# A two-layer diffusion backbone on one core: constant products ahead of the first stage, weights stored by partition, and value products with the softmax sum in one bank

## The chip, the cores and the metric

The kernel runs on one core of a Trainium2 chip. The metric is the device time of one execution in microseconds (us). Three runs of the kernel before took 1395.3, 1395.98 and 1396.6 us, so the median is 1395.98 us.

## What is computed

The input is a latent stream `x` of 1024 tokens, a context of 256 tokens, both 1024 wide in fp32, and a conditioning vector. Two layers follow, and an RMS norm at the end. Each layer normalises its input, scales and shifts it by a modulation vector (a product of the conditioning with a 1024 x 3072 matrix), projects it, runs attention, multiplies by a SiLU gate and projects back.

```python
mod_x = (silu_c @ w_mod[i] + b_mod[i])
hx = rms_norm(x, norm_g[i]) * (1.0 + sc_x) + sh_x
# layer 0: 16 query heads on 4 key/value heads, q and k normed, rotary positions on latent tokens
s = jnp.einsum('bqkgd,bskd->bkgqs', qi, k_all).astype(jnp.float32) * ATTN_SCALE
p = jax.nn.softmax(s, axis=-1)
o = jnp.einsum('bkgqs,bskd->bqkgd', p, v_all)
yx = (o * jax.nn.silu(z)) @ w_out
# layer 1: 16 heads, an 8 x 16 neighbourhood with a learned bias, and the context keys
x = x + g_x * yx
```

Layer 0 also updates the context, with attention among the context tokens alone. In the title and in the kernel "layer one" of the change is this layer 0, the grouped attention.

## The kernel before, in words

Tokens stand in ten tiles of 128: t = 0 to 7 are latent, 8 and 9 context. To keep fp32 accuracy each fp32 operand is split into a high and a low fp16 part, and each product is made of three fp16 products (high by high, high by low, low by high) that add up in PSUM.

**First stage.** `mod_cols(kt)` loads one column block of the modulation matrix (four DMAs into two tiles `wm`, in runs of 128 floats), multiplies it by the conditioning (`pm`, L552), copies the result (`mrow`, L554), turns it into columns (`pmc`, L557) and leaves scale `acol` (L558) and shift `scol` (L560). `ln_pre(t)` loads a token tile and divides it by its root mean square. `h_kt(t0, n, kt)` transposes n tiles of block kt on TensorE (L791), applies scale and shift on ScalarE into an fp32 tile `tf` (L793), casts that to the high part on VectorE (L796) and subtracts for the low part (L797). `kv_mm` (L801) makes the key and value projection: 24 products of 512 columns for each token tile. Tiles 0 to 3 go through kt = 0 to 7 together, each in a PSUM bank of its own; tiles 4 to 9 follow. `kv_post` norms and rotates the keys and writes `k1`, `k2`, `v1`. In `v1` each head has 64 high columns, one column with a constant (for the softmax sum) and 64 low columns.

**Layer 0.** A pair u of heads goes through `a_proj` (q and gate, L917; the q tiles are transposed by DMA, L934, two token tiles at a time, and copied, L936), then `a_att` and, for u = 0 to 3 and the latent tiles, also `q_att` for the second head. `a_att` has keys on the partitions, needs a row of maxima beforehand (`mgen`, `rows`), and multiplies probabilities by values in `pv_mm`: for each key tile and each of up to four query tiles, three products: high by `v[0:65]` (L1014), high by `v[65:129]` (L1015), low by `v[0:65]` (L1016). `o_evict` divides by the sum (L992 to L996). `q_att` has queries on the partitions; it takes its sums from the accumulator of the Exp on ScalarE (L1086), transposes its probabilities by DMA (L1088), multiplies by 128 value columns (L1094) and 64 (L1096), and finishes with a reduction, a copy, an addition and four scaled products (L1105 to L1112). `o_out` splits the head pair's output and transposes each part by its own DMA (L1027). `mod_block` computes the other modulation vectors (L571, L579) spread over the layer.

**Layer 1** loads its weights in `b_load` (64 DMAs, in runs of 128 floats, L1304), projects (`b_qk` L1322, `b_vz` L1355, L1358), runs attention in `b_att` and finishes each half of a head in `fin` (L1446 to L1456), which also calls `o_out`. `b_out` ends the kernel (L1527).

**Order.** All DMAs but four small ones are issued by SyncE (SP), one after the other. The function calls of the program only set a first rank. The class `Planner` gives each instruction a cost, builds the dependences between tiles, simulates the five engines, derives due times and repeats that five times; the best order that it finds is then fixed on every engine. On each engine the chip runs the instructions in that order, and so does the SP queue.

Of the kernel before, what the change touches and what calls it, by code (L numbers as in the profile page):

```python
# [21 lines left out]
P = 128  # L22
# [20 lines left out]
class Planner:  # L43
# [42 lines left out]
    def cost(self, x, rd, wr):  # L86
# [67 lines left out]
    def graph(self):  # L154
        acc = {}
        self.pred = []
        self.node = []
# [11 lines left out]
        for x in self.ins:  # L169
# [11 lines left out]
            p = set()  # L181
# [29 lines left out]
            self.pred.append(p)  # L211
        self.eng = [self.ENG[x.engine.name] for x in self.node]
# [42 lines left out]
    def schedule(self, key=None, margin=0.0, scale=None):  # L255
# [4 lines left out]
        succ = [[] for _ in range(N)]  # L260
        npred = [0] * N
        for i, ps in enumerate(self.pred):
            npred[i] = len(ps)
            for p in ps:
                succ[p].append(i)
        rdy = [0.0] * N
# [143 lines left out]
        self.order, self.start, self.done, self.succ, self.came = order, start, done, succ, came  # L410
        return max(done)

    def deadlines(self, margin):
# [14 lines left out]
        for i in sorted(range(N), key=lambda i: -start[i]):  # L428
            e, d = self.eng[i], done[i] - start[i]
            for j in self.succ[i]:  # L430
                due[i] = min(due[i], due[j] - (0.0 if self.eng[j] == e == "PE" else d + self.SEM[self.eng[j]] + margin))
            for j in heirs.get(i, ()):
# [46 lines left out]
def trunk_kernel(ctx, tc, x, cx, cc, norm_g, ng_row, b_cols, sel_c, w_mod, b_mod, a_w_in, a_qg, a_kg, a_w_out,  # L479
                 b_w_in, rpb, b_w_out, fin_g, cos_t, sin_t, mask_q, out):  # L480
# [17 lines left out]
    def ps_pv(name):  # L498
        return psum.tile([P, 4, 65], F32, name=name, tag="pv", bufs=2)
# [41 lines left out]
    def mod_cols(kt, pool):  # L541

        tiles = []
        for j in range(2):
            wm = pool.tile([P, 4, 2, P], F32, name=f"wm{kt}{j}", tag="wm", bufs=7)
# [3 lines left out]
            tiles += [wm[:, d] for d in range(4)]  # L549
        ps = ps_mx(f"pm0{kt}", shape=(P, 2, P))  # L550
        for d in range(KT):
            T.matmul(ps[32 * (d % 4):32 * (d % 4) + 32], s2[:, d, :], tiles[d], start=d < 4, stop=d >= 4)  # L552
        row = lp.tile([P, 2, P], F32, name=f"mrow{kt}", tag="mrow", bufs=1)
        V.tensor_copy(row, ps)  # L554
        pc = ps_mx(f"pmc0{kt}", shape=(P, 2, 2))
        for r in range(2):
            T.matmul(pc[:, r, :], row[:, r, :], sel, start=True, stop=True)  # L557
        V.tensor_scalar(acol[0][:, kt, :], pc[:, 1, :], hg[:, 0, kt:kt + 1], gb[:, 0, kt:kt + 1], op0=ALU.mult,  # L558
                        op1=ALU.add)
        V.tensor_scalar(scol[0][:, kt, :], pc[:, 0, :], 0.5, bsc[:, 0, 0, kt:kt + 1], op0=ALU.mult, op1=ALU.add)  # L560

    def mod_block(pool, l, c0):
# [4 lines left out]
        for hf in range(2):  # L567
            wm = pool.tile([P, KT // 2, 512], F32, name=f"wg{nm}{hf}", tag="wg", bufs=1)
            for i in range(KT // 2):
                kt = hf * KT // 2 + i  # L570
                DM.dma_start(wm[:, i], w_mod[l, kt * P:(kt + 1) * P, c0:c0 + 512])  # L571
                yield 1.0
# [93 lines left out]
    oc_hi = yp.tile([P, KT, NC * P], F16, name="oc_hi")  # L666
    oc_lo = yp.tile([P, KT, NC * P], F16, name="oc_lo")
# [31 lines left out]
    def norm_rope_split(pool, sqs, psv, alt, nt, nh, t0, gc, gs, gplain, nm):  # L699
# [29 lines left out]
        q16 = pool.tile([P, 4, 2, HD], F16, name="q16" + nm, tag="q16", bufs=2)  # L729
# [16 lines left out]
    def a_src(kt0, nk, ncol):  # L746
# [869 lines left out]
```

## Time and profile before

| | |
|---|---|
| median of three runs | 1395.98 us |
| profiled execution, own time | 1397.8 us |
| its span, first to last instruction | 1396.0 us |
| TensorE (PE) busy | 1341.6 us, 96% |
| weight loads (PEld) busy | 930.8 us, 67% |
| VectorE (DVE) busy | 1000.0 us, 72% |
| ScalarE (ACT) busy | 938.8 us, 67% |
| GpSimd (POOL) busy | 648.5 us, 46% |
| queue of SP: packets, MB | 433544, 178.66 |

Busy is the time in which at least one instruction of the engine was under way. Products on TensorE overlap: the next begins while the one before still drains, so the distance between two starts, not the duration of one, is what a product costs in a full stream. 1.8 us of the profiled execution lie outside its span.

### The profile page before, as it was taken

To read this page: it belongs to the slowest core of one execution; us is meant where nothing else is said; L and a number is where in the kernel's file an instruction comes from. 1 tells how busy PE (TensorE), PEld (TensorE's weight loads), DVE (VectorE), ACT (ScalarE), POOL (GpSimd) and SP (SyncE) were. 2 spreads that over 40 slices of the span, in tenths; PEclk is the share of its full clock that TensorE was granted. 3 is DMA by queue.
4 is the path that set the end of the run, shared out by engine and by line. 5 is a ranking of instruction groups with operands and counts; after the bars stand their busy time and mean duration, and the time that the engine had idled before them with its cause. 6 is when DMAs were issued, how large, how long until landed. Compare 5 with 4: busy or idle time off the path is not lost.

```text
span 1396.0 us, 35447 instructions
## 1 busy us (share of the span) xinstructions
PE 1341.6 (96%) x13402; PEld 930.8 (67%) x13402; DVE 1000.0 (72%) x2568; ACT 938.8 (67%) x2294; POOL 648.5 (46%) x907
## 2 busy tenths in 40 slices
PE   4899999999999999999999999999999999999897
PEld 2458777777777777776654476867677686867443
DVE  2697878888789787689347756677776768687733
ACT  2463889888979777788742437677777767686811
POOL 2132778776867766687864301312122222322332
PEclk9999999999999999999999999999999999999999
DMA  8754468778676223234438735585666766597832
GB/s 258 234 125 118 98 120 134 141 151 159 139 142 136 70 62 70 57 111 109 104 97 192 188 97 114 94 157 122 128 136 116 144 112 148 97 170 149 172 109 103
DMA packets 434294, 180.97 MB, mean 130 GB/s; under 512 B 340225, under 2 KB 412865, under 8 KB 434121
## 3 DMA queue, kind: packets, MB, share of 16 engines
q1 hardware_dynamic: 433544, 178.66, 58.5%
q8 instruction: 105, 1.72, 0.5%
q14 instruction: 69, 0.56, 0.1%
q10 hardware_dynamic: 576, 0.03, 0.0%
HBM read 87.36 MB, written 12.08 MB: 71 GB/s over the span
## 4 chain that ended last, share of the span: by engine, by line
PE 56%; DVE 8%; ACT 5%; issue 3%; DMA 2%; POOL 0%; DVEq 0%; POOLq 0%; ACTq 0%; SPq 0%
PE pvz L1355 11%; PE poa L1236 7%; PE pa L917 7%; PE pb L1322 6%; PE pob L1527 5%; PE st L1143 3%; PE st L1144 2%; PE pm L947 2%; PE pv L1015 2%; PE pv L1014 2%; PE pv L1016 2%; PE bpv L1435 1%; ACT bpf L1426 1%; PE pvz L1358 1%; DVE bmx L1413 1%
## 5 line engine op out<-in xcount | busy, mean ns | idle before, releaser
L1008 POOL TENSOR_TENSOR pl<-pf,ph 128x256 f16<-128x256 f32 x400 | 273.6, 708 | 77.7 <-ACT pf L1130 61.9
L1008 POOL TENSOR_TENSOR bph<-bpf,bph 128x256 f16<-128x256 f32 (+1 forms) x128 | 99.6, 789 | 314.5 <-ACT bpf L1426 245.8
L917 PE MATMUL pa<-wa,x 128*128 128x256 f16 x1536 | 220.3, 272 | 1.0 <-DVE q16q L731 0.6
L1322 PE MATMUL pb<-hb_hi,wb 128*128 128x512 f16 (+1 forms) x640 | 191.4, 358 | 0.7 <-DVE bq L1337 0.7
L1128 ACT ACTIVATE ph<-st 128x512 f16<-128x512 f32 x240 | 143.9, 603 | 59.2 <-PE st L1144 56.2
L1355 PE MATMUL pvz<-wb,hb_hi 128*128 128x256 f16 x1024 | 174.8, 273 | 4.9 <-DVE bk L1341 3.3
L917 PEld LDWEIGHTS <-x 128*128 128x128 f16 x1536 | 140.0, 97 | 33.6 <-issue 2.5
L948 DVE TENSOR_REDUCE mxp<-pm 128x1 f32<-128x512 f32 x192 | 128.8, 684 | 25.9 <-PE pm L947 24.9
L1130 ACT ACTIVATE pf<-st 128x512 f32<-128x512 f32 x240 | 144.4, 605 | 0.3
L1322 PEld LDWEIGHTS <-wb 128*128 128x128 f16 x960 | 92.9, 98 | 75.0 <-issue 1.3
L1355 PE MATMUL pvz<-wb,hb_lo 128*128 128x256 f16 x512 | 139.7, 273 | 0.0
L1015 PE MATMUL pv<-v,ph 128*128 128x64 f16 x960 | 123.8, 195 | 0.0
L1014 PE MATMUL pv<-v,ph 128*128 128x65 f16 x960 | 123.4, 193 | 0.0
L1016 PE MATMUL pv<-v,pl 128*128 128x65 f16 x960 | 122.1, 192 | 0.6 <-POOL pl L1008 0.6
L1355 PEld LDWEIGHTS <-hb_hi 128*128 128x128 f16 x1024 | 97.1, 98 | 29.2 <-DVE bk L1341 5.1
L1008 POOL TENSOR_TENSOR qpp<-qpf,qpp 128x256 f16<-128x256 f32 (+1 forms) x158 | 93.7, 617 | 47.7 <-ACT qpf L1086 35.3
L1322 PE MATMUL pb<-hb_lo,wb 128*128 128x512 f16 (+1 forms) x320 | 114.6, 358 | 0.0
L1014 PEld LDWEIGHTS <-ph 128*128 128x128 f16 x960 | 90.9, 97 | 20.8 <-issue 0.6
L1015 PEld LDWEIGHTS <-ph 128*128 128x128 f16 x960 | 90.4, 97 | 15.2
L1016 PEld LDWEIGHTS <-pl 128*128 128x128 f16 x960 | 91.2, 99 | 10.9 <-POOL pl L1008 1.6
L1424 ACT ACTIVATE bph<-bpf,bnx 128x384 f16<-128x384 f32 (+1 forms) x128 | 68.6, 581 | 39.1 <-DVE bnx L1416 38.9
L1143 PE MATMUL st<-q,k 128*128 128x512 f16 x240 | 90.9, 379 | 0.9 <-ACT pf L1130 0.7
(261 smaller groups left out, 3678.9 us busy)
## 6 DMA issues: line engine op xcount, KB each, us to landing
wg<-in_w_mod SPq DMA_DIRECT2D x64, 256.0 KB
wsb<-in_b_w_in SPq DMA_DIRECT2D x64, 256.0 KB
wm<-in_w_mod SPq DMA_DIRECT2D x32, 256.0 KB
wsa<-in_a_w_in SPq DMA_DIRECT2D x64, 128.0 KB
xstage<-in_x SPq DMA_DIRECT2D x8, 512.0 KB
wsoa<-in_a_w_out SPq DMA_DIRECT2D x16, 256.0 KB
x<-in_x SPq DMA_DIRECT2D x8, 512.0 KB
x_d<-x SPq DMA_DIRECT2D x8, 512.0 KB
```

The lines of the kernel that those rows point to most:

```text
L917: T.matmul(ps[:, :, i, :], hA(a, kt, t), wt[w][:, kt, :], start=n == 0, stop=n == 3 * KT - 1)
L948: V.tensor_reduce(mxs[i][:, t, ch:ch + 1], pm, axis=AX.X, op=ALU.max)
L1008: G.tensor_tensor(lo[:, c], p32[:, c], hi[:, c], op=ALU.subtract)
L1014: T.matmul(pv[:, t, :], hi[:, c], v[:, 0:65], start=first and t == 0, stop=False)
L1015: T.matmul(pv[:, t, 0:HD], hi[:, c], v[:, 65:129], start=False, stop=False)
L1016: T.matmul(pv[:, t, :], lo[:, c], v[:, 0:65], start=False, stop=last and t == n - 1)
L1128: S.activation(ph, st, AF.Exp)
L1130: S.activation(p32, st, AF.Exp)
L1143: T.matmul(so, k1[:, g, kc], q1[:, :, i, :], start=True, stop=False)
L1236: T.matmul(ps, lhs(a, kt), w[b][:, kt, :], start=n == 0, stop=n == 3 * KT - 1)
L1322: T.matmul(ps[:, 0:n].rearrange("p (t q) -> p t q", q=P), wt[a][:, kt, which * P:(which + 1) * P], hb[b][:, c0 // P:(c0 + n) // P, kt], st ...
L1355: T.matmul(ps[:, :, j, :], hb[a][:, t, kt], wt[w][:, kt, 256:512], start=m == 0, stop=m == 3 * KT - 1)
```

## The change

The weights are laid out beforehand so that each partition reads one long run. The first stage works on tile 4 together with tiles 0 to 3 (three blocks behind), and computes the modulation of later blocks ahead. 34 products of a constant tile stand in front of it. `h_kt` writes the high part directly from ScalarE and makes an fp32 copy on VectorE from PSUM. In layer 0 the accumulator of a query tile takes a place of 129 columns (65 for the fourth), so that high by `v[0:129]` is one product; `q_att` uses the same products and takes its sum from the constant column. High and low parts are transposed by one DMA where there were two, and from u = 1 on four q tiles by one. The planner's cost of a DMA falls by 15%, and a second DMA into the same tile no longer waits, in the plan, for the first to land.

```diff
@@ Planner.cost, graph
-            return (430.0 if len(list(outs[0].ap)) < 3 else 550.0), m * 4 / ro * (11 + ro * 0.0432) / 16
+            return (430.0 if len(list(outs[0].ap)) < 3 else 550.0), m * 4 / ro * (11 + ro * 0.0432) / 16 * 0.85
...
-                            p.add(r[1])
+                            (o if self.ENG[x.engine.name] == self.ENG[self.node[r[1]].engine.name] == "SP"
+                             else p).add(r[1])
@@ mod_cols: split into load, quarters, cols
-            for r in range(2):
-                a = w_mod[0, 4 * j * P:4 * j * P + P, r * D + kt * P:r * D + kt * P + 1]
-                DM.dma_start(wm[:, :, r, :], bass.AP(a.tensor, a.offset, [[3 * D, P], [P * 3 * D, 4], [1, P]]))
+                DM.dma_start(wm, w_m0[kt, :, 4 * j:4 * j + 4])
@@ mod_block
-                DM.dma_start(wm[:, i], w_mod[l, kt * P:(kt + 1) * P, c0:c0 + 512])
+                DM.dma_start(wm[:, i:i + 2], w_mb[n, :, kt:kt + 2])
@@ first stage
+    ones = lp.tile([P, 512], F16, name="ones")
+    V.memset(ones, 1.0)
+    idle = ps_mx("idle")
+    for n in range(34):
+        T.matmul(idle, ones[:, 0:P], ones, start=n == 0, stop=n == 33)
@@ h_kt
-        S.activation(tf[:, 0:n], ps, AF.Identity, scale=acol[0][:, kt, s:s + 1], bias=scol[0][:, kt, s:s + 1])
-        V.tensor_copy(hi[:, kt, c], tv)
-        V.tensor_tensor(lo[:, kt, c], tv, hi[:, kt, c], op=ALU.subtract)
+        S.activation(hi[:, kt, c], pv, AF.Identity, scale=a, bias=b)
+        V.tensor_scalar(tf, pv, a, b, op0=ALU.mult, op1=ALU.add)
+        V.tensor_tensor(lo[:, kt, c], tf, hi[:, kt, c], op=ALU.subtract)
@@ main loop of the first stage
+    LAG = 3
+    for kt in range(KT + LAG):
+        if kt + 2 < KT:
+            loads(kt + 2)
...
+        if kt < KT:
+            kv_mm(banks[0], 0, kt)
+        if kt + 1 < KT:
+            mod[kt + 1][2]()
+            h_kt(0, 4, kt + 1)
+        if kt < KT:
+            for t in range(1, 4):
+                kv_mm(banks[t], t, kt)
+        if kt + 2 < KT:
+            mod[kt + 2][1]()
+        if kt >= LAG:
+            h_kt(4, 1, kt - LAG)
+            kv_mm(banks[4], 4, kt - LAG)
+        if kt >= KT:
+            kv_post(banks[kt - KT], kt - KT)
+        if kt >= 5:
+            h_kt(5, 3, kt - 5)
@@ a_load
-            load_w(wa[u], a_src(2 * j, 2, [u * P, 1536 + u * P]), 2 * j, 2, 256, f"a{u}{j}")
+            load_w(wa[u], a_src(a_wq[u, :, 2 * j:2 * j + 2].rearrange("p k r c -> p (k r c)")), 2 * j, 2, 256, f"a{u}{j}")
@@ b_load
-                DM.dma_start(st.rearrange("p (r c) -> p r c", c=P),
-                             bass.AP(a.tensor, a.offset, [[4 * D, P], [D, 4], [1, P]]))
+                DM.dma_start(st, b_wp[u, :, kt].rearrange("p r c -> p (r c)"))
@@ a_proj.post
+            if u and b in (0, 2):
+                return
+            c = slice(0 if u else 2 * (b % 2), 2 * (b % 2) + 2)
@@ o_evict
+        lo = pool.tile([P, 3, HD], F32, name="olo" + nm, tag="olo", bufs=1)
+        S.copy(lo[:, 0:m], pv_cols(pv, HD + 1, m, HD))
+        V.tensor_tensor(pv_cols(pv, 0, m, HD), pv_cols(pv, 0, m, HD), lo[:, 0:m], op=ALU.add)
@@ pv_mm
-            T.matmul(pv[:, t, :], hi[:, c], v[:, 0:65], start=first and t == 0, stop=False)
-            T.matmul(pv[:, t, 0:HD], hi[:, c], v[:, 65:129], start=False, stop=False)
-            T.matmul(pv[:, t, :], lo[:, c], v[:, 0:65], start=False, stop=last and t == n - 1)
+        o = 129 * t
+        if t < 3:
+            T.matmul(pv[:, o:o + 129], hi, v[:, 0:129], start=first, stop=False)
+        else:
+            T.matmul(pv[:, o:o + 65], hi, v[:, 0:65], start=first, stop=False)
+            T.matmul(pv[:, o:o + HD], hi, v[:, 65:129], start=False, stop=False)
+        T.matmul(pv[:, o:o + 65], lo, v[:, 0:65], start=False, stop=last)
@@ o_out
-            for dst, src in ((hi, oh), (lo, ol)):
-                DM.dma_start_transpose(dst[:, c].rearrange("p (t q) -> p t q", q=P),
-                                       src[:, 0:n].rearrange("p t f -> p (t f)"))
+            DM.dma_start_transpose(dst.rearrange("p t a q -> p (t a) q"), oo[:, 0:n].rearrange("p t a f -> p (t a f)"))
@@ q_att
-                S.activation(pf, pf, AF.Exp, bias=nmx, accum_out=sums[:, t, c:c + 1])
+                S.activation(pf, pf, AF.Exp, bias=nmx)
...
-        V.tensor_reduce(sm, sums, axis=AX.X, op=ALU.add)
-        V.tensor_scalar_mul(sm, sm, 2.0 * WS * WS)
-        V.reciprocal(sm, sm)
...
-        S.copy(oc, pv[:, :, HD:P])
-        V.tensor_tensor(oc, pv[:, :, 0:HD], oc, op=ALU.add)
-        for t in range(4):
-            V.scalar_tensor_tensor(og[:, t, HD:P], oc[:, t], sm[:, t:t + 1], sz[:, t, HD:P], op0=ALU.mult, op1=ALU.mult)
+        o_evict(aq, pv, og, 4, sz, 0, 1, f"q{u}{pt_}")
@@ b_att.fin
-                    for t in range(4):
-                        V.scalar_tensor_tensor(og[:, t, i * HD:(i + 1) * HD], oc[:, t], sm[:, t:t + 1],
-                                               sz[:, hf * 4 + t, i * HD:(i + 1) * HD], op0=ALU.mult, op1=ALU.mult)
+                    V.tensor_tensor(oc, oc, sm.unsqueeze(2).broadcast_to([P, 4, HD]), op=ALU.mult)
+                    V.tensor_tensor(og[:, :, i * HD:(i + 1) * HD], oc, sz[:, hf * 4:hf * 4 + 4, i * HD:(i + 1) * HD],
+                                    op=ALU.mult)
```

## Rows read from the trace of the kernel before

**Rows 1.** Busy time of each engine by stage: stretch, length, PE, PEld, DVE, ACT, POOL.
```profile
117.00:450.00 333.00, 323.43 (x3992) 249.62 (x3990) 275.05 (x766) 269.51 (x625) 237.17 (x362) 1.00 0.68 134
450.00:690.00 240.00, 238.83 (x3181) 175.06 (x3179) 176.31 (x370) 189.76 (x380) 179.87 (x254) 1.00 0.35 86
...
800.00:1300.00 500.00, 491.69 (x4489) 360.20 (x4487) 359.91 (x1026) 354.25 (x1024) 120.42 (x169) 1.00 0.65 129
```

**Rows 2.** The chain that ended last: start, length, what (two of its pieces).
```profile
718.88 64.55 PE poa L1236 x299
...
839.25 2.68 PE pvz L1358 x48
```

**Rows 3.** PE in order of time in the first stage: start, length, line.
```profile
11.79 0.69 PE L791 MATMUL pl<-idf,xstage 128*128 128x128 f32 x2 [11.79 <-DVE ms_ln L604]
...
26.14 4.60 PE L801 MATMUL pkv<-wkv,x 128*128 128x512 f16 x11
...
61.19 1.07 PE L552 MATMUL pm<-wm,s 128*32 128x256 f32 x16
...
62.81 0.61 PE L557 MATMUL pmc<-sel,mrow 128*128 128x2 f32 x4 [0.18 <-DVE ms_ln L604]
63.27 2.75 PE L801 MATMUL pkv<-wkv,x 128*128 128x512 f16 x12
65.86 0.71 PE L791 MATMUL pl<-idf,xstage 128*128 128x128 f32 x5
...
100.33 0.39 PE L811 MATMUL pkt<-id,q16k 128*128 128x128 f16 x4
...
109.41 0.60 PE L917 MATMUL pa<-wa,x 128*128 128x256 f16 x4
```

**Rows 4.** Stretches of 10 us in the first stage: columns as in rows 1, then clock, DMA share, GB/s.
```profile
10.00:20.00 10.00, 5.13 (x27) 2.40 (x28) 3.87 (x9) 3.56 (x8) 2.21 (x4) 1.00 1.08 313
...
50.00:60.00 10.00, 7.93 (x44) 3.85 (x45) 5.50 (x15) 6.50 (x11) 1.96 (x3) 0.83 1.07 371
...
90.00:100.00 10.00, 10.00 (x58) 5.38 (x57) 9.88 (x32) 6.22 (x15) 3.05 (x3) 1.00 0.32 87
```

**Rows 5.** PE in order of time in layer 0: nine value products and what follows.
```profile
506.15 0.19 PE L1014 MATMUL pv<-v,ph 128*128 128x65 f16 x1
...
506.43 0.38 PE L947 MATMUL pm<-k,q 128*128 128x512 f16 x1
```

**Rows 6.** Groups by line and form: count, busy us, mean ns, idle before.
```profile
L1453 DVE SCALAR_TENSOR_TENSOR bog<-boc,bse,bsz 128x64 f32<-128x64 f32 x128 | 37.5, 341 | 0.2
L1086 ACT ACTIVATION_READ_ACCUMULATOR qpf<-qpf,qnx 128x1 f32 x96 | 19.6, 204 | 0.0
L1240 DVE TENSOR_TENSOR tm<-poa,gt 128x512 f32<-128x512 f32 x20 | 13.8, 688 | 18.5 <-PE poa L1236 18.4
L1450 ACT COPY boc<-bpv 128x256 f32<-128x256 f32 x32 | 12.0, 374 | 15.8 <-PE bpv L1437 15.7
L1112 DVE SCALAR_TENSOR_TENSOR og<-qoc,qse,sz 128x64 f32<-128x64 f32 x32 | 11.7, 408 | 0.0
L994 DVE TENSOR_TENSOR pv<-pv,ors 128x256 f32<-128x256 f32 x24 | 10.2, 427 | 0.4
L796 DVE CAST x<-tf 128x512 f16<-128x512 f32 x16 | 8.4, 525 | 4.7 <-ACT tf L793 4.6
```

**Rows 7.** Who waited for whom: total us, times, longest (whole span; SP queue among them).
```profile
PEld L1094 <- DMA qpp<-qpp: 7.1, 9, 1.9
...
SPq L1304 <- DVE bv L1366: 25.9, 2, 25.7
...
SPq L548 <- PE pm L552: 14.8, 5, 5.3
```

**Rows 8.** SP in order of time in layer 0: start, length; first and last of 40.
```profile
347.14 1.22 SPq L1027 DMA_TRANSPOSE oa<-oh  x1
...
394.34 1.20 SPq L1027 DMA_TRANSPOSE oc_hi<-oh2c  x1
```

More of the change, by code (lines that the diff above doesn't have):

```diff
@@ L156, in graph @@
         self.pred = []
+        self.after = []
         self.node = []
@@ L260, in schedule @@
         succ = [[] for _ in range(N)]
+        late = [[] for _ in range(N)]
         npred = [0] * N
         for i, ps in enumerate(self.pred):
-            npred[i] = len(ps)
+            npred[i] = len(ps) + len(self.after[i])
             for p in ps:
                 succ[p].append(i)
+            for p in self.after[i]:
+                late[p].append(i)
         rdy = [0.0] * N
@@ L409, in schedule @@
                     offer(j)
-        self.order, self.start, self.done, self.succ, self.came = order, start, done, succ, came
+            for j in late[i]:
+                rdy[j] = max(rdy[j], s)
+                npred[j] -= 1
+                if not npred[j]:
+                    offer(j)
+        self.order, self.start, self.done, self.succ, self.late, self.came = order, start, done, succ, late, came
         return max(done)
@@ L498, in ps_pv @@
     def ps_pv(name):
-        return psum.tile([P, 4, 65], F32, name=name, tag="pv", bufs=2)
+        return psum.tile([P, 512], F32, name=name, tag="pv", bufs=2)
     idf = main.tile([P, P], F32, name="idf")
@@ L562, in mod_block, with load, quarters @@
-    def mod_block(pool, l, c0):
+        def load():
+            for j in range(2):
+                wm = pool.tile([P, 4, 2, P], F32, name=f"wm{kt}{j}", tag="wm", bufs=7)
+                DM.dma_start(wm, w_m0[kt, :, 4 * j:4 * j + 4])
+                tiles.extend(wm[:, d] for d in range(4))
+        def quarters():
+            ps = ps_mx(f"pm0{kt}")
+            pm = ps[:, 0:2 * P].rearrange("p (a b) -> p a b", a=2)
+            for d in range(KT):
+                T.matmul(pm[32 * (d % 4):32 * (d % 4) + 32], s2[:, d, :], tiles[d], start=d < 4, stop=d >= 4)
+            row = lp.tile([P, 2, P], F32, name=f"mrow{kt}", tag="mrow", bufs=1)
+            V.tensor_copy(row, pm)
+            tiles[:] = [ps, row]
@@ new lines, in cols @@
+        def cols():
+            ps, row = tiles
+            pc = ps[:, 2 * P:2 * P + 4].rearrange("p (a b) -> p a b", a=2)
+            for r in range(2):
+                T.matmul(pc[:, r, :], row[:, r, :], sel, start=True, stop=True)
+            V.tensor_scalar(acol[0][:, kt, :], pc[:, 1, :], hg[:, 0, kt:kt + 1], gb[:, 0, kt:kt + 1], op0=ALU.mult,
+                            op1=ALU.add)
+            V.tensor_scalar(scol[0][:, kt, :], pc[:, 0, :], 0.5, bsc[:, 0, 0, kt:kt + 1], op0=ALU.mult, op1=ALU.add)
@@ L564, in mod_block @@
+        return load, quarters, cols
+    def mod_block(pool, n, l, c0):
         nm = f"{l}{c0}"
@@ L842, in trunk_kernel @@
     tc.swap_default_side()
-    for kt in range(KT):
-        h_kt(4, 4, kt)
-        if kt % 2:
-            kv_post(banks[kt // 2], kt // 2)
+    for kt in range(KT + LAG - 5, KT):
+        h_kt(5, 3, kt)
+    for t in range(3, 5):
+        kv_post(banks[t], t)
     wa = {}
@@ L861, in trunk_kernel @@
         if t < NX:
-            for kt in (2 * t - 8, 2 * t - 7):
+            for kt in range((8, 11, 14)[t - 5] - 8, (11, 14, 16)[t - 5] - 8):
                 h_kt(8, 2, kt)
@@ L1058, in q_att @@
         pend = []
-        pv = psum.tile([P, 4, P], F32, name=f"qpv{u}{pt_}", tag="pv", bufs=2)
-        sums = aq.tile([P, 4, 3], F32, name=f"qsm{u}{pt_}", tag="qsm", bufs=2)
+        pv = ps_pv(f"qpv{u}{pt_}")
         og = og_of(u, pt_)
```

185 lines of the change are left out of this document (87 added, 98 removed).

## The prediction

> **What bounds it now.** I read the busy times by stage first [rows 1]. In both attention stages of layer 0 and in layer 1 TensorE is busy for 97 to 99% of the stretch, every other engine less: 9.6 us are open at 117 to 450 us, 1.2 at 450 to 690, 8.3 in layer 1. So I asked whether a busy TensorE is a full one. In the chain that ended last, 299 products of 512 columns take 64.55 us, 0.216 each, and 48 of 128 columns 2.68 us, 0.056 each [rows 2]: one distance between starts, column by column, with nothing in between. There TensorE bounds the kernel, and only fewer columns or fewer products help.
>
> The Trainium skill, "Trainium Kernel Development and Optimization", section Performance Expectations, says that matmul busy time is a bad metric, and that the busy share of weight loads is a good one. By that, with weight loads at 75% of the stretch from 117 to 450 us, a quarter of TensorE's time would be free, the term for value products below would be 0, and the time 1374 instead of 1369. I go by the starts.
>
> The first stage is different. The first product starts at 11.79 us, and layer 0's projection at 109.41 [rows 3]. TensorE's own work in it, at full rate: 240 key and value products at 0.216 = 51.8 us; 80 transposes at 0.11 (five of them take 0.71, of which 0.27 is the last one's length) = 8.8; eight modulation blocks at 1.07 and their columns at 0.61 = 13.4; ten key transposes of 0.39, some 0.25 of it before the next product, = 2.5. That is 76.5 us of 109.4; 33 are lost. Three losses show. Nothing runs until 11.8 us. Eleven products then take 4.60 us, 0.43 each, the 1.2 GHz level, where later twelve take 2.75 [rows 3]. And block by block TensorE waits for modulation, ScalarE and VectorE, while loads wait in turn for `pm` to free their buffers, 14.8 us [rows 7]: the DMAs move 313 and 371 GB/s where they run [rows 4], but don't run throughout.
>
> **The change, part by part.**
>
> *First stage.* The constant products need no load. 34 of them take 7.3 us at 0.216 or 14.6 at 0.43; from about 1 us they end between 8.5 and 15.6. I take 12.5, as a part of them runs at the lower level. By then the first modulation block (1 MB), the first token tile (0.5 MB) and the first weights (0.25 MB) have landed: 1.75 MB at 313 GB/s are 5.6 us, behind some 2 us of issue. Real work starts near 13 us. Loads are no bound after that: until the last block 8.4 MB of modulation weights, 4.2 of tokens and 2.1 of projection weights are 14.7 MB, 47 us at 313 and 40 at 371 GB/s, while TensorE's eight steps of the loop (1.68 modulation, 0.55 transposes, 15 x 0.216 products = 5.5 us) take 44. With 76.5 us of work and no loss the stage would end at 89.5. I add 3.5 us for waits, as each block still passes TensorE, VectorE, TensorE, VectorE and ScalarE one after the other, now a step ahead of its use: **93 instead of 109.4, -16.4 us**. Bounds: 87.5 (work from 11, no loss, -22) and 103 (VectorE, first rival, -6). VectorE gets more work here: the cast of 525 ns gives way to a pass from PSUM like the 688 of L1240 [rows 6], 0.16 more for each of 16 blocks of four tiles and about as much again for smaller pieces, some 4 us. What hides it is TensorE's own loop; VectorE is busy 9.88 of 10 us at 90 to 100 us [rows 4], so that cover is thin.
>
> *Value products of layer 0.* Nine take 0.28 us, 0.093 for three [rows 5]. A product of 129 columns costs 0.056 by rows 2, one of 65 a third of 0.093, so two cost 0.087: 6 ns less. Three products become two in 240 key tiles x 3 query tiles and 16 x 2 x 2 of the context, 784 times: -4.9 us. In `q_att` the first three query tiles cost one column more, nothing; the fourth takes three products for two, 80 times 6 ns = +0.5. **-4.4 us**, on TensorE's full stream. Bounds: 0 (129 columns as dear as the two they replace) and -8.
>
> *Evictions and sums.* `q_att` loses 96 accumulator reads of 204 ns on ScalarE, 19.6 us, and, per block, four products of 408 ns against two of 427 [rows 6] on VectorE, eight times. All 40 evictions of `a_att` gain a copy and an addition: about 0.32 and 0.36 us for 192 columns by the 374 and 427 of 256 columns, 24 times, and some 0.27 and 0.29 for 128, 16 times: 25 us in all, half on each engine. I cost it at nothing: two PSUM banks take turns, and TensorE has the products of the other one and the projections. If that cover is gone, all 25 us return and the time is near 1394. ScalarE's balance in the first half, where it is busiest, is better by over 10 us; that shortens waits only where TensorE waits, so nothing is booked.
>
> *DMA queue.* In layer 0 the SP queue is nearly always issuing: 40 issues in the 48 us from 347.14 on, a transpose 1.2 us whatever its size [rows 8]. Gone are 14 of 40 transposes of q and 21 of 42 of outputs (14 in layer 0's latent part, 7 in the context's), 42 us of issue time, and 78 shorter issues: 14 copies of q, 32 of 64 weight loads and 32 of 64 modulation loads. What waits for the queue now is `q_att`'s value product, 7.1 us [rows 7]. I take **-4 us**, between 0 and -7.1, since buffers also hold the queue. q tiles 0 and 1 now leave with tiles 2 and 3; the maxima of all four were needed by the same row of maxima before, so nothing further waits for it.
>
> *Layer 1.* Four products of 341 ns [rows 6] become two of about 0.42, 32 times: 17 us less of VectorE; 14 fewer transposes, and longer runs for 64 loads. TensorE is open for 8.3 us here [rows 1]. I take **-2 us**, between 0 and -8.3.
>
> **Sum.** The profiled execution took 1397.8 us: -16.4 - 4.4 - 4 - 2 = -26.8 gives 1371.0. It lies 1.8 above the median of the runs, so the forecast is 1369 us. All lower bounds together give 1350, all upper ones 1390.
>
> **Rivals.**
>
> *VectorE bounds the first stage.* It is full at 90 to 100 us already, 9.88 of 10 [rows 4], with some 4 us to come. Against: it idles half of the first 60 us, which the loop now fills. The stage ends at 103: 10.4 us more, 1379.
>
> *The clock falls again.* The constant products raise it, but TensorE then waits for loads and for its first block. For: it was granted 0.83 at 50 to 60 us, after TensorE had waited between blocks [rows 4]. At 0.43 a product until about 30 us, some 8 us are lost: 1377. The Trainium skill, "TensorE: Matmul & The Clock Gate", HAM oscillation, says that waits for DMA throttle TensorE anew; by that page constant products that end before the loads land are in vain. The 0.83 agrees.
>
> *The head start is lost.* Layer 0 begins earlier, but keys of the last tiles wait for VectorE, and TensorE runs out of projection work: 16 us come back, with the other terms halved 1390. Against: 25 us of projection stand between.
>
> *Slower: a load at the head of the queue.* The plan now lets a second DMA into a tile go at once and holds transfers cheaper, so it may put weight loads earlier. On the chip a load whose buffer is still read holds every later transpose. The nearest price: L1304 waited 25.7 us once [rows 7]. TensorE has some 2 us of value products pending, so each such wait within attention costs about 24. From two on the gain is gone: 1369 + 48 = 1417. Against: the longest waits now fall where nothing hangs on the queue.
>
> **How the numbers follow.** Forecast 0.64, its own range 1358 to 1381; VectorE 0.14; clock 0.09; head start 0.06; queue 0.07. From 1356 to 1388 lie nearly nine tenths of the first and the next two, some 0.8. Within 0.2% (2.8 us, about what a measurement of this kernel can tell from no change) lies half of the head start's case: 0.03. Faster: 0.90; slower: 0.07.
>
> **What would show it.** Right: layer 0's projection starts near 93 us; products at 0.216 from about 12 us on; three value products in 0.087 us; `q_att` waits less than 4 us for transposes; layer 1's fins lose 17 us of VectorE. Wrong: VectorE full and TensorE open at 60 to 100 us; value products of 129 columns well over 0.06; waits of PE for evictions, or a long wait of a load at the head of SP while transposes stand behind it.

## The result, and the profile after

The changed kernel takes **1383.4 us** (median of four runs, 1381.65 to 1386.41) against 1395.64 for the kernel before: a ratio of 0.9914, 95% interval 0.9895 to 0.9932. The forecast was 1369, with a range from 1356 to 1388: the sign and the range held, the gain is 12 us instead of 27. One execution of the kernel before in the series below (1746.55 us) and one of the changed kernel (1872.02 us) ran at a lower granted clock (0.75 and 0.73) and are left out of every median and ratio. The profiled execution took 1382.83 us with a span of 1381.0, 15.0 us shorter than the span before.

The first stage, PE in order of time (start, length, line):

```profile
1.47 10.39 PE L772 MATMUL idle<-ones 128*128 128x512 f16 x34 [1.47 <-DVE twos L552]
11.70 0.38 PE L807 MATMUL pl<-idf,xstage 128*128 128x128 f32 x2
...
93.56 5.27 PE L965 MATMUL pa<-wa,x 128*128 128x256 f16 x46
...
116.68 1.01 PE L999 MATMUL pm<-k,q 128*128 128x512 f16 x2 [2.38 <-issue]
...
121.21 0.38 PE L1191 MATMUL st<-q,k 128*128 128x512 f16 x1
```

Layer 0's projection starts at 93.56 us instead of 109.41 [rows 3]: the 15.8 us are there. Ahead of 116.68 TensorE has waited 2.38 us, the first long wait of the projection. Stretches of 10 us (columns as in [rows 4]) show what the stage now runs against:

```profile
10.00:20.00 10.00, 8.02 (x67) 4.29 (x66) 6.28 (x20) 5.06 (x10) 1.41 (x2) 1.00 1.03 408
50.00:60.00 10.00, 7.82 (x42) 3.97 (x40) 9.38 (x22) 8.43 (x19) 6.95 (x6) 1.00 0.54 71
60.00:70.00 10.00, 9.72 (x57) 5.25 (x57) 9.94 (x26) 5.79 (x13) 2.32 (x3) 1.00 0.60 157
90.00:100.00 10.00, 10.00 (x82) 7.39 (x80) 9.44 (x24) 5.30 (x13) 3.47 (x4) 1.00 0.38 120
110.00:120.00 10.00, 7.53 (x51) 5.47 (x50) 4.92 (x12) 1.47 (x4) 1.01 (x1) 0.83 0.75 114
```

First the loads are full (DMA share 1.03, 408 GB/s), then VectorE is (9.4 to 9.9 of 10 us); the clock falls at the wait near 115 us. The stages after that, with the columns of [rows 1], are as full as they were, 323.87 and 238.23 us of TensorE against 323.43 and 238.83:

```profile
117.00:450.00 333.00, 323.87 (x3741) 246.81 (x3743) 271.89 (x746) 268.64 (x550) 234.34 (x358) 0.99 0.65 130
450.00:690.00 240.00, 238.23 (x2751) 171.12 (x2740) 176.72 (x380) 193.42 (x398) 183.49 (x259) 1.00 0.30 84
...
800.00:1300.00 500.00, 491.98 (x4544) 364.01 (x4545) 359.50 (x996) 360.06 (x1045) 127.14 (x172) 1.00 0.65 131
```

Where did the head start go? Layer 1's first product, in the kernel before and then in the changed one (PE in order of time):

```profile
793.61 0.38 PE L1322 MATMUL pb<-hb_hi,wb 128*128 128x512 f16 x1
```
```profile
784.21 0.38 PE L1372 MATMUL pb<-hb_hi,wb 128*128 128x512 f16 x1
```

From the first projection to here, layer 0 took 793.6 - 109.4 = 684.2 us before and 784.2 - 93.6 = 690.6 after: **+6.4, where -8.4 was forecast**. From here to the end of the span it is 602.4 before and 596.8 after, -5.6. So -15.8 + 6.4 - 5.6 = -15.0.

For layer 0 I use one account throughout. For every product, the time by which the next one starts later than the median distance of its form counts as **waits** (over 12 ns, at full clock) or as **clock** (at the lower one); the rest is the **stream**, what TensorE needs if nothing is late. The fp32 products of the modulation, whose distances alternate between short and long, count as stream. Before: stream 666.0, waits 18.2, clock 0. After: stream 662.0, waits 23.6, clock 5.0. The stream lost the 4 us that the value products were to give; waits and clock took 10.4.

Groups (columns as in [rows 6]) and waits (as in [rows 7]) of the changed kernel:

```profile
L1503 DVE TENSOR_TENSOR bog<-boc,bsz 128x256 f32<-128x256 f32 x32 | 16.6, 520 | 0.5
...
L1502 DVE TENSOR_TENSOR boc<-boc,bse 128x256 f32<-128x256 f32 x32 | 14.4, 449 | 0.2
...
L1056 DVE TENSOR_TENSOR pv<-pv,olo 128x192 f32<-128x192 f32 x24 | 8.7, 362 | 5.3 <-ACT olo L1055 5.2
...
L1055 ACT COPY olo<-pv 128x192 f32<-128x192 f32 x24 | 7.8, 325 | 0.8 <-DVE ors L1051 0.6
```
```profile
PEld L1079 <- DMA qpp<-qpp: 2.9, 4, 1.0
...
PEld L1077 <- DMA qpp<-qpp: 2.1, 4, 1.0
...
PE pm L999 <- issue: 2.4, 1, 2.4
...
PE st L1191 <- ACT pf L1178: 1.4, 3, 0.7
```

The copy and the addition take what was worked out, 0.33 and 0.36 us. `q_att` waits 2.9 + 2.1 = 5.0 us for transposes instead of 7.1. The value products run as forecast (PE in order of time):

```profile
480.63 0.22 PE L1077 MATMUL pv<-v,ph 128*128 128x129 f16 x1
480.69 0.19 PE L1081 MATMUL pv<-v,pl 128*128 128x65 f16 x1
480.71 0.22 PE L1077 MATMUL pv<-v,ph 128*128 128x129 f16 x1
...
480.88 0.19 PE L1079 MATMUL pv<-v,ph 128*128 128x65 f16 x1
```

Three places take 0.25 us, 0.083 each where three products took 0.093 [rows 5].

### The profile page after: what moved, and what is told of

It reads as the page before. It is cut to its first block, busy times and chain, and to the rows that moved or that the text cites. A ratio compares the mean times of both kernels' runs of the same rounds, so it can differ in the third digit from the quotient of the medians.

```text
span 1381.0 us, 33811 instructions
## 1 busy us (share of the span) xinstructions
PE 1345.3 (97%) x12732; PEld 931.0 (67%) x12732; DVE 1008.1 (73%) x2535; ACT 943.6 (68%) x2249; POOL 651.7 (47%) x907
## 4 chain that ended last, share of the span: by engine, by line
PE 84%; DVE 7%; ACT 3%; DMA 3%; issue 2%; POOL 1%; SPq 0%; DVEq 0%; POOLq 0%; ACTq 0%
PE pb L1372 13%; PE pa L965 12%; PE pvz L1405 12%; PE poa L1288 8%; PE pob L1576 5%; PE st L1191 3%; PE st L1192 3%; PE pv L1077 3%; PE pkv L818 3%; PE pm L999 2%; PE bpv L1485 2%; PE pv L1081 2%; DVE mxp L1000 2%; PE pvz L1408 1%; DMA qpp<-qpp 1%
## 5 line engine op out<-in xcount | busy, mean ns | idle before, releaser
L965 PE MATMUL pa<-wa,x 128*128 128x256 f16 x1536 | 225.9, 273 | 0.7 <-DVE q L753 0.5
L965 PEld LDWEIGHTS <-x 128*128 128x128 f16 x1536 | 143.6, 98 | 39.1 <-issue 1.6
L1077 PE MATMUL pv<-v,ph 128*128 128x129 f16 x720 | 106.8, 222 | 0.0
L1192 PE MATMUL st<-q,k 65*128 65x512 f16 x240 | 91.4, 381 | 0.0
L1288 PE MATMUL poa<-woa,oa 128*128 128x512 f16 x384 | 91.0, 379 | 0.0
L1576 PE MATMUL pob<-wob,ob 128*128 128x512 f16 x384 | 86.2, 379 | 2.9 <-DVE bmx L1456 1.5
```

Of the source, the lines that this page charges most:

```text
L965: T.matmul(ps[:, :, i, :], hA(a, kt, t), wt[w][:, kt, :], start=n == 0, stop=n == 3 * KT - 1)
L1077: T.matmul(pv[:, o:o + 129], hi, v[:, 0:129], start=first, stop=False)
L1192: T.matmul(so, k2[0:65, g, kc], q2[0:65, :, i, :], start=False, stop=True)
L1288: T.matmul(ps, lhs(a, kt), w[b][:, kt, :], start=n == 0, stop=n == 3 * KT - 1)
L1576: T.matmul(ps, ob[kt][:, t, a], wout["b"][hf][b][:, kt, :], start=n == 0, stop=n == 3 * KT - 1)
```

## Experiments

The ratios are to the kernel before, timed beside each run.

**The first stage.** Without the constant products:

```diff
-    ones = lp.tile([P, 512], F16, name="ones")
-    V.memset(ones, 1.0)
-    idle = ps_mx("idle")
-    for n in range(34):
-        T.matmul(idle, ones[:, 0:P], ones, start=n == 0, stop=n == 33)
```

> Leaves out the 34 constant products, nothing else. If they raise the clock in time: the first real products run at 0.43 us for 512 columns instead of 0.216 until about 25 to 30 us, and the projection of layer 0 starts near 100 instead of 93.6 us; time 1388 to 1391. If they only fill a wait for the loads: projection at 93 to 95 us, time 1382 to 1385.

1378.2 us, ratio 0.9862 (0.9836 to 0.9888). PE in order of time, and two stretches (columns as in [rows 4]):

```profile
16.88 1.94 PE L568 MATMUL pm<-wm,s 128*32 128x256 f32 x16
```
```profile
92.53 4.66 PE L959 MATMUL pa<-wa,x 128*128 128x256 f16 x40
```
```profile
10.00:20.00 10.00, 8.40 (x47) 3.51 (x48) 5.71 (x16) 3.84 (x8) 1.41 (x2) 1.00 1.02 408
20.00:30.00 10.00, 10.00 (x81) 5.55 (x80) 5.87 (x16) 3.70 (x7) 0.55 (x1) 1.00 1.03 404
```

The second modulation block starts at 16.88 us at the lower clock (1.94 us, where it takes 1.07 in the changed kernel, which starts it at 16.90): the loads set this pace, at 408 and 404 GB/s. The projection starts a microsecond earlier, not later. The constant products buy nothing here.

`h_kt`'s second pass, the one in fp32, on ScalarE:

```diff
-        V.tensor_scalar(tf, pv, a, b, op0=ALU.mult, op1=ALU.add)
+        S.activation(tf, pv, AF.Identity, scale=a, bias=b)
```

> The fp32 copy of h_kt is written by ScalarE instead of VectorE, which takes some 14 us off VectorE in the first 90 us. If VectorE's backlog eats the head start: the projection starts at 91 to 94 us as before, but the first product of the maxima moves from 116.7 to 110 to 113 us, and the time falls by 3 to 6 us, to 1377 to 1380. If loads ahead of the first transposes of q, or something later, eat it: first product of the maxima at 115 to 117 us, time 1382 to 1385.

1378.5 us, ratio 0.9868 (0.9846 to 0.9890). The stretches and the first score product (PE in order of time):

```profile
90.00:100.00 10.00, 10.00 (x88) 7.93 (x87) 7.42 (x18) 4.06 (x10) 2.12 (x3) 1.00 0.45 134
100.00:110.00 10.00, 10.00 (x94) 8.98 (x92) 5.68 (x15) 2.64 (x8) 4.34 (x8) 1.00 0.47 140
```
```profile
116.11 0.38 PE L1191 MATMUL st<-q,k 128*128 128x512 f16 x1
```

The projection starts at 92.65, only 0.9 us earlier, so VectorE did not set the end of the stage. But with VectorE at 7.4 and 5.7 instead of 9.4 and 9.3 of 10 us, the first score product comes 5.1 us earlier, and the 4.1 us that TensorE waits in the first 40 us of the projection are gone. That fits a backlog of VectorE that goes into layer 0's start, but does not show it: in the run without constant products VectorE is as full as in the changed kernel (9.67 and 8.95 of 10 us in the same two stretches), TensorE waits 0.9 us in those 40, and the first score product comes earlier still:

```profile
115.48 0.38 PE L1185 MATMUL st<-q,k 128*128 128x512 f16 x1
```

In the changed kernel's own second profile (shown below) it comes at 118.83.

The gate's loads behind the first transposes of q. In the changed kernel those transposes stand behind some 2 MB of weight and gate loads (SP in order of time):

```profile
110.28 3.30 SPq L987 DMA_TRANSPOSE q<-q  x2
116.39 1.14 SPq L988 DMA_DIRECT2D q<-q  x2
```

```diff
+        gate = {i for i in sp if type(self.node[i]).__name__ == "InstDmaTransposeAnt" and name(i).startswith("q100")}
+        for i in sp:
+            if name(i).startswith("wg02048"):
+                self.after[i] |= gate
```

> Holds the loads of the first gate block in the SP queue behind the first two transposes of q. If the loads in front of them delay these transposes: they land 2 to 3 us earlier, the first product of the maxima is at 113 to 115 instead of 116.7 us, and the time falls by 2 to 3 us. If VectorE's backlog is the cause: the first product of the maxima moves by less than 1 us, and the time stays within 1.5 us of 1383.

1378.1 us, ratio 0.9865 (0.9840 to 0.9889); the first score product at 117.1, the early waits 1.5 instead of 4.1 us. But layer 0 as a whole took 688.9 us, and 688.9 and 688.6 in the two runs above, between the 687.4 and 690.6 of the changed kernel's two profiles (the second is of the next run): no gain is left at the end of layer 0. The three end some 5 us lower all the same. Against the mean of those two profiles, 2.4 to 3.3 of the 3.7 to 4.9 us by which their spans are shorter lie behind layer 1's first product, in a part that none of them touches.

> The changed kernel as it is, once more, beside the variants of it that follow. The variants without constant products, with the old value products, with the copy on ScalarE and with the gate loads held back all took 1377 to 1378 us, about 5 below the 1383.4 of the changed kernel, though they undo quite different things. If those 5 us are theirs, this run gives 1383 again. If they are of the chip or of the neighbouring kernels, it gives 1378 here, and then none of the four edits is worth anything by itself except what a stage of its trace shows.

1384.0 us, ratio 0.9905 (0.9891 to 0.9920): the 5 us are the variants' own. What they share is that the planner, given any other instruction, writes another order for all that follows.

**The old value products.** The changed kernel with the whole value part of before (products, sums, evictions):

```diff
-        T.matmul(pv[:, o:o + 129], hi, v[:, 0:129], start=first, stop=False)
+        T.matmul(pv[:, t, :], hi[:, c], v[:, 0:65], start=first and t == 0, stop=False)
+        T.matmul(pv[:, t, 0:HD], hi[:, c], v[:, 65:129], start=False, stop=False)
...
-        S.copy(lo[:, 0:m], pv_cols(pv, HD + 1, m, HD))
-        V.tensor_tensor(pv_cols(pv, 0, m, HD), pv_cols(pv, 0, m, HD), lo[:, 0:m], op=ALU.add)
...
-                S.activation(pf, pf, AF.Exp, bias=nmx)
+                S.activation(pf, pf, AF.Exp, bias=nmx, accum_out=sums[:, t, c:c + 1])
```

> The changed kernel with the value products, evictions and sums of layer 0 as before (three products for two 784 times, accumulator reads on ScalarE). If TensorE's stream bounds the attention of layer 0: 4.4 us longer, 1388. If the attention is held by waits on other engines: within 2 us of 1383.

1377.1 us, ratio 0.9851 (0.9826 to 0.9875), faster than the changed kernel, which neither theory expected (two further orders of it, below, are not). Layer 0's ends (PE in order of time):

```profile
93.88 5.19 PE L965 MATMUL pa<-wa,x 128*128 128x256 f16 x46
```
```profile
776.85 0.38 PE L1367 MATMUL pb<-hb_hi,wb 128*128 128x512 f16 x1
```

That is 683.0 us: stream 666.2, as before, but waits 16.7. Next I took away the copy and the addition of the evictions alone, so that the low half's contribution is left out:

```diff
-        S.copy(lo[:, 0:m], pv_cols(pv, HD + 1, m, HD))
-        V.tensor_tensor(pv_cols(pv, 0, m, HD), pv_cols(pv, 0, m, HD), lo[:, 0:m], op=ALU.add)
```

> The new value products of layer 0 stay, but the evictions lose the copy of the low half on ScalarE and the addition on VectorE: the contribution of the weights' low half is left out of the first three query tiles of each block. Theory (the evictions are not covered: the copy and the addition delay the freeing of the value banks and hold the two engines while TensorE waits): the stretch from the first layer-0 projection to the first layer-1 product shortens from 690 to 683 us or less, and the time is 6 to 9 us below the changed kernel's. Rival (the loss lies in the products of 129 columns, or in the order): the stretch stays at 689 to 691 and the time within 2 us.

1379.3 us, ratio 0.9883 (0.9864 to 0.9901), between the two theories. Waits are still 23.6 us; what went is the time at the lower clock. Then the edit of the old value products for one attention at a time, `q_att` alone (its copy `oc` in the one buffer of `olo`, which both attentions share in the changed kernel too) and `a_att` alone:

> Only the row-maximum attention gets its old value products, accumulated sums and eviction back (80 key tiles); the other attention keeps places of 129 columns and its eviction with copy and addition. With all of the old value products TensorE's stream in layer 0 is 4 us longer, but its waits are 7 us shorter. Theory A (the longer hold of the value bank in the row-maximum attention, whose eviction now reads the bank in five steps, causes the waits): the waits of TensorE between layer 0's first projection and layer 1's first product fall from 23.6 to about 17 us at a stream of 662, and the time is 1377 to 1379 us. Theory B (ScalarE, VectorE and GpSimd set the pace of the other attention, so that a shorter stream only waits longer): nothing changes, waits stay at 22 to 25 us, the time within 2 us of the changed kernel's 1384.

1389.0 us, ratio 0.9960 (0.9945 to 0.9975): waits 31.1, clock 4.2, stream 662.4.

> The counterpart: only the attention without row maxima gets its old three value products of 65, 64 and 65 columns and its old eviction back (256 key and context tiles), the row-maximum attention keeps the new ones. Theory A: the waits stay near 24 us and the stream grows to 666, so the time is 1386 to 1388. Theory B: the stream grows to 666 us, the waits fall to 16 to 18 us, and the time is 1377 to 1380, below the changed kernel's.

1388.6 us, ratio 0.9954 (0.9941 to 0.9968): waits 29.5, stream 666.9. Both theories missed, with one order tried for each half: giving back either half made it slower, giving back both made it faster. The streams are near what was worked out, though: `a_att`'s new products give 666.2 - 662.4 = 3.8 or 666.9 - 662.0 = 4.9 us, `q_att`'s between -0.7 and 0.4.

**The order alone.** One number of the planner, the margin of its due times; every instruction stays.

```diff
-        plan.refine(5, 100.0, 300.0)
+        plan.refine(5, 100.0, 320.0)
```

> The changed kernel with one number of its planner changed (320 instead of 300 ns as the margin of the due times): the same instructions, in another order. It measures how far the order alone moves the time. If the planner's order is worth little, it is within 1.5 us of the changed kernel in the same call; if the order is the reason why unlike edits all come out near 1378, it differs by 3 to 8 us, most likely below, and every difference of that size between variants is then no evidence for the edit by itself.

> The changed kernel with a margin of 280 ns: a third order of the new value products. Waits of 23 to 30 us and 1382 to 1388 if they go with the products; 15 to 19 us and 1375 to 1379 would show that a good order of the new ones exists and that the order was to blame.

> The changed kernel with the old value products, evictions and sums, planned with a margin of 320 ns. If the waits go with the value products, they stay at 15 to 19 us (16.7 with the margin of 300) and the time at 1375 to 1380, some 8 us below the 1387.8 of the changed kernel under the same margin. If the order decides, the waits are 23 us or more and the time 1383 or above.

> The same with a margin of 280 ns: a third order of the old value products. Waits of 15 to 19 us and 1375 to 1380 if they go with the products, 23 or more and 1383 or above if the order decides.

> The kernel before with 320 instead of 300 ns as the margin of the planner's due times: the same instructions in another order. It says how far the order alone moves the kernel before. If the waits go with the value products, TensorE's waits between layer 0's first projection and layer 1's first product stay at 15 to 20 us (18.2 before) and the time within 4 us of before's. If the order decides, they may be 23 us and more, and the time 1400 or above.

| kernel, margin | us | ratio (interval) | layer 0 | waits | clock |
|---|---|---|---|---|---|
| changed, 280 | 1379.4 | 0.9886 (0.9870 to 0.9902) | 689.1 | 23.5 | 3.5 |
| changed, 300 | 1384.0 | 0.9905 (0.9891 to 0.9920) | 687.4 | 23.7 | 1.7 |
| changed, 320 | 1387.8 | 0.9931 (0.9916 to 0.9946) | 693.6 | 29.9 | 1.6 |
| old values, 280 | 1378.1 | 0.9880 (0.9862 to 0.9897) | 686.1 | 20.6 | 0 |
| old values, 300 | 1377.1 | 0.9851 (0.9826 to 0.9875) | 683.0 | 16.7 | 0 |
| old values, 320 | 1385.1 | 0.9928 (0.9915 to 0.9941) | 693.5 | 23.4 | 1.9 |
| before, 300 | 1395.6 | 1 | 684.2 | 18.2 | 0 |
| before, 320 | 1390.6 | 0.9962 (0.9948 to 0.9975) | 683.5 | 15.6 | 1.6 |

The order alone moves each kernel by 5 to 8 us by the medians, 5 to 11 by the ratios. And the old value products are faster than the new ones under 300 alone: under 280 and 320 the intervals of the two overlap almost wholly (0.9880 and 0.9886, 0.9928 and 0.9931). The kernel before under 320 starts its projection 8 us earlier (PE in order of time; 109.41 in [rows 3]):

```profile
101.20 0.60 PE L917 MATMUL pa<-wa,x 128*128 128x256 f16 x4
```

So about half of the first stage's gain could be had from another order of the old stage. The planner's old rules in the changed kernel:

```diff
-            ... / 16 * 0.85
+            ... / 16
...
-                            (o if self.ENG[x.engine.name] == self.ENG[self.node[r[1]].engine.name] == "SP"
-                             else p).add(r[1])
+                            p.add(r[1])
```

> The changed kernel with the planner's old rules: a second transfer into a tile waits for the first one in the plan, and transfers are costed at the full rate. If the new rules let the queue run ahead and that is worth something, the time rises by 3 to 8 us, with waits for transposes and loads in layer 0. If they are neutral, it is within the 3 us by which another order alone moved the changed kernel. If loads put early at the head of the queue cost time in the changed kernel, it falls below 1381.

1379.7 us, ratio 0.9888 (0.9870 to 0.9906), 4.2 us below the changed kernel by the medians, 2.4 by the ratios. Its projection starts 3 to 4 us later, at 97.6; layer 0 takes 687.0 us with waits of 23.3, like the changed kernel's. The new rules bring no measurable gain; that the old ones are better is not shown, as this is one order each.

**The order kept.** Two edits that leave each instruction where it was on every queue: the planner is told the old sizes. First a longer stream, the low half's product with 14 more columns in 1024 places (they add a term far below the others):

```diff
-        T.matmul(pv[:, o:o + 65], lo, v[:, 0:65], start=False, stop=last)
+        T.matmul(pv[:, o:o + (79, 65)[t == 3]], lo, v[:, 0:(79, 65)[t == 3]], start=False, stop=last)
```

> The changed kernel, every instruction in the same order: the low half's value product takes 79 instead of 65 columns in 1024 places, with the planner still told 65. 14 columns at 0.216 us per 512 are 5.9 ns each, 6.0 us of TensorE in layer 0. If TensorE is the bound there, the time rises by all 6 us, to 1390, and the waits stay at 23.6 us. If ScalarE, VectorE and GpSimd set the pace and a shorter stream only waits longer (the theory for the lost 4 us), the waits fall by 4 to 6 us and the time by no more than 2 us from 1384.

1388.1 us, ratio 0.9948 (0.9928 to 0.9969): 4.1 us more than the changed kernel by the medians, 0.0043 x 1395 = 6.0 by the ratios. Layer 0's ends, first of the changed kernel's second profile, then of this one:

```profile
94.70 5.27 PE L965 MATMUL pa<-wa,x 128*128 128x256 f16 x46
```
```profile
782.08 0.38 PE L1372 MATMUL pb<-hb_hi,wb 128*128 128x512 f16 x1
```
```profile
94.54 5.27 PE L965 MATMUL pa<-wa,x 128*128 128x256 f16 x46
```
```profile
786.78 0.38 PE L1372 MATMUL pb<-hb_hi,wb 128*128 128x512 f16 x1
```

687.4 against 692.2 us: stream 668.1, 6.1 more; waits 22.4, 1.3 less; clock 1.8 against 1.7. In this order TensorE is the bound; a shorter stream does not just wait longer. Then thin evictions (63 of 64 columns of the low half are left out):

```diff
-        S.copy(lo[:, 0:m], pv_cols(pv, HD + 1, m, HD))
+        S.copy(lo[:, 0:m, 0:1], pv_cols(pv, HD + 1, m, 1))
```

> The changed kernel, every instruction in the same order: the copy and the addition of the 40 evictions take one column of each query tile instead of 64 (the low half's contribution is left out in the other 63), with the planner still told 64. By the 192 columns that they lose, some 0.2 us each on ScalarE and VectorE, 14 to 18 us in all. If the evictions are hidden behind TensorE, as the prediction has it, the time stays within 2 us of the changed kernel's 1384. If their cover is gone, TensorE's waits in layer 0 fall by 5 us or more and the time with them.

1381.8 us, ratio 0.9905 (0.9884 to 0.9925), the changed kernel's own ratio, and 2.2 us less by the medians. All 40 copies and additions (duration min/median/max in ns):

```profile
L1055 ACT COPY olo<-pv x40: 141/165/317, 157.9 to 708.2; 128x3 f32<-128x3 f32 x24, 128x2 f32<-128x2 f32 x16
L1056 DVE TENSOR_TENSOR pv<-pv,olo x40: 152/164/170, 158.2 to 708.4; 128x3 f32<-128x3 f32 x24, 128x2 f32<-128x2 f32 x16
```

From medians of 319 and 356 ns to 165 and 164: 14 us less work, and layer 0 takes 689.9 us with 26.3 of waits: no gain there. The work of the evictions is hidden, to within the 2.2 us.

**Layer 1.** The four scaled products of before:

```diff
-                    V.tensor_tensor(oc, oc, sm.unsqueeze(2).broadcast_to([P, 4, HD]), op=ALU.mult)
-                    V.tensor_tensor(og[:, :, i * HD:(i + 1) * HD], oc, sz[:, hf * 4:hf * 4 + 4, i * HD:(i + 1) * HD],
-                                    op=ALU.mult)
+                    for t in range(4):
+                        V.scalar_tensor_tensor(og[:, t, i * HD:(i + 1) * HD], oc[:, t], sm[:, t:t + 1],
+                                               sz[:, hf * 4 + t, i * HD:(i + 1) * HD], op0=ALU.mult, op1=ALU.mult)
```

> The changed kernel with the four scaled products per block of layer 1 instead of two wide ones: 32 times some 0.5 us more of VectorE, 17 us in all. If these set what layer 1 gained (from its first product to the first output product 493.0 us before, 486 to 490 in the variants after), that stretch is back at 492 to 494 and the time is 4 to 6 us above the changed kernel's. If the merged transposes and longer loads gave it, or the plan's order, the stretch stays at 486 to 490 and the time within 2 us.

1387.6 us, ratio 0.9950 (0.9934 to 0.9966), 3.7 us above the changed kernel by the medians, 6.3 by the ratios. Its group, and its first layer-1 and output products:

```profile
L1503 DVE SCALAR_TENSOR_TENSOR bog<-boc,bse,bsz 128x64 f32<-128x64 f32 x128 | 35.8, 330 | 0.3
```
```profile
783.77 0.38 PE L1372 MATMUL pb<-hb_hi,wb 128*128 128x512 f16 x1
```
```profile
1275.93 2.75 PE L1576 MATMUL pob<-wob,ob 128*128 128x512 f16 x12
```

The stretch is 492.2 us, against 487.4 and 489.0 in the changed kernel's two profiles and 493.0 before. This is again a new order, but in all seventeen profiles with the wide products the stretch took 485.8 to 490.6 us, so the run lies outside what orders alone gave: the two wide products carry most of layer 1's gain.

**Four edits together**: no constant products, old value part, fp32 pass on ScalarE, gate loads held back.

> Four edits together: no constant products, old value products with their evictions and sums, the fp32 copy of the first stage on ScalarE, the gate loads behind the first transposes of q. If the four gains add (first stage 1 to 2 us, layer 0 6 us, start of attention 1 to 2 us), the time is 1371 to 1374 us, the fastest version. If the order of the plan makes up the differences, it is 1376 to 1379 like each of them alone.

**1374.0 us** (1372.95 to 1377.96), ratio 0.9841 (0.9826 to 0.9856), the fastest: layer 0 in 680.8 us with 15.2 of waits, and once risen the clock falls nowhere before the last products. It was run in one order only; how much of its lead is the order's was not tried.

## Why the prediction was wrong

*What bounds the kernel: right.* Read by starts, TensorE was full. With the order kept, 6.1 us more stream made layer 0 4.8 us longer. By the Trainium skill's page "Trainium Kernel Development and Optimization" (Performance Expectations), a quarter of its time was free; the runs side with the starts.

*First stage, -16.4: right,* -15.8 and -14.7 in two profiles, but partly for another reason. "Loads are no bound after that" is wrong: they run at 401 to 408 GB/s from 10 to 40 us, and the constant products raise a clock that the loads then don't need. The rival in which VectorE ends the stage at 103 fell. The rival in which the head start is lost came true in part: 4.1 us of waits and 1.6 of clock in the first 40 us of the projection (2.2 and 0 in the second profile, 0.9 and 0 before), where "25 us of projection stand between" was to cover them.

*Clock, put at nothing: this failed in layer 0.* The lower clock near 50 us is gone, as forecast. But in layer 0 falls cost 5.0 us in the first profile and 1.7 in the second, and the sum has no term for them. Behind the constant products the first profile shows no fall in the first stage; the second shows one at 15.5 us, lasting 3.4 us. Either way these products bought nothing. The Trainium skill's page "TensorE: Matmul & The Clock Gate" (HAM oscillation) would have them undone by waits for loads. They were in vain, but without them the stage ended no later, so the clock was not what counted. The fall near 50 us in the kernel before, with which the prediction saw that page agree, came in a wait of 1.39 us for ScalarE's `tf` (L793), by the profile, and not for a load.

*Value products, -4.4: right* for the stream, which fell from 666.0 to 662.0 in layer 0. The time did not follow (see the sum).

*Evictions and sums, 0: right* for the evictions within what the runs can tell, 0 to 2.2 us; the sums were not tried by themselves.

*Layer 1, -2: mis-sized.* It gave 5.6 us, 4.0 in the second profile. VectorE's busy time fell by 37.5 - 31.0 = 6.5 us, not 17. Some 4 us of the difference is the price of the wide products (449 and 520 ns, not 420). The other 6 is a wrong reading of [rows 6]: the 128 old products overlap, so that they were busy for 37.5 us and not for 128 x 341 ns = 43.6. But more of what was left lay on TensorE's path. That was luck: without it the miss would be 3.6 us larger, 2.0 in the second profile.

*DMA queue, -4: this step failed.* The waits of `q_att` for transposes did fall by 2.1 us, to 5.0 (its sign was under 4). But the forecast booked that as fewer waits in all. In layer 0 TensorE's waits rose instead, from 18.2 to 23.6 us in the first and 23.7 in the second profile: 9.4 us above the forecast. Even with the old value products, where everything else of the change is in place, layer 0 waits 16.7 to 23.4 us in three orders, against 15.6 and 18.2 before. Where TensorE waits less for transposes, it waits for something else, as here between 95 and 660 us in the kernel before, and then with the old value products under 280. There it waits for the row of maxima that ScalarE writes into `q` (L1040); the kernel before has no such wait in that stretch:

```profile
PE qpv L1094 <- DMA qpp<-qpp: 4.8, 7, 1.5
```
```profile
PE qs L1117 <- ACT q L1040: 2.4, 2, 1.6
PE qpv L1142 <- DMA qpp<-qpp: 2.2, 3, 0.9
```

The rival of a load that stands at the head of the queue did not come. The longest that a load held SP in layer 0 is 8.8 us, for output weights issued between 514.7 and 638.0 us, and TensorE is busy for 238.23 of the 240 us around them:

```profile
SPq L1236 <- DVE woa L662: 25.3, 6, 8.8
```

*The sum: this step failed by more.* It added terms as if the order around them stood still. The planner writes the whole order anew for any edit. In eight orders of the changed kernel's value products (the three above, and those without constants, with the fp32 pass moved, with loads held back, with old rules, with old fins) layer 0 waits 23 to 30 us; in six orders with old ones 15 to 23. That difference, some 7 us by the means (25.3 and 18.3), and 2.9, 7.0 and 6.5 us margin by margin in the changed kernel, is more than the 4 us of stream. So layer 0 as a whole is no shorter for the new products: 3.0, 4.4 and 0.1 us longer margin by margin. What makes them wait more stays open. With the order kept, neither the stream nor the work of the evictions accounts for it. What is left are the orders drawn for the new products, or a dependence of the new products themselves that no run took out alone, such as the sums from the constant column; giving back one attention made it worse still, and no run kept an order of the old products for the new ones. The gain of 12 us is itself one pair of orders: by the means over the margins tried it is 1393.1 - 1383.7 = 9 us.

## What to carry to other kernels

Where a planner writes the order, time the same instructions under two or three other orders before you credit an edit: here that alone moved the median by 5 to 8 us, as much as most of the terms. To price one term, keep the order: change the work of an instruction and let the planner see the old size. And a stage that starts earlier is worth only what the next one can take up: look at the next one's first waits.

## What was unexpected of the hardware

The clock falls differently in two executions of one order. The changed kernel's second profile, stretches around the places where its first one showed falls at 116.6, 287.2 and 434.0 us (columns as in [rows 4]):

```profile
110.00:120.00 10.00, 9.44 (x81) 7.59 (x79) 8.00 (x20) 2.25 (x7) 1.01 (x1) 1.00 0.42 115
285.00:292.00 7.00, 6.33 (x106) 4.68 (x108) 5.87 (x21) 6.77 (x15) 4.40 (x6) 1.00 0.46 105
432.00:440.00 8.00, 7.61 (x99) 6.22 (x99) 6.60 (x20) 6.90 (x15) 4.52 (x7) 0.79 0.18 35
```

Only the third fell (0.79). Where the first profile fell at 116.6, TensorE had just waited 2.38 us; at 287.2 it had waited 0.57 and 0.75 us in the microseconds before, and the second profile shows the same two waits without a fall. A fall of 3.4 us at half speed (0.83 over 10 us) costs 1.6 to 1.8 us, so the three make up 5.0 us of the profiled execution's layer 0.
